# Strided casts shared with GpSimd, the state copy in eight pieces, and four kinds of preparation moved or cut smaller in a decode step

## The chip, the cores and the metric

The kernel runs on one core of a Trainium2 chip. The metric is the device time of one execution in microseconds (us). TensorE does the matrix products, VectorE, ScalarE and GpSimd the elementwise work, and SyncE's queue issues nearly all data transfers (DMAs), in order.

## What is computed

One layer of a decoder in one inference step: a prompt of 1024 tokens (8 tiles of 128) and 32 sample tokens (8 sequences of 4 tokens, each with 1024 cached positions). Two groups of attention heads stand in parallel, and their outputs are gated, projected and added to the input.

```python
u = h @ w_in            # all projections of the normalized input
# NSA: 8 query heads in 2 groups, three branches over shared keys/values
cmp_kv = compress_blocks(kv_c, cmp_pos, w_cmp1, w_cmp2)      # 32-row blocks, stride 16
logit_c = einsum(q, cmp_k) * scale + bias_c                   # compressed branch
logit_s = einsum(q, k_sel) * scale + bias_s                   # selected branch
logit_w = einsum(q, win_k) * scale + bias_w                   # window of 512
o_nsa = g0 * softmax(logit_c) @ v_c + g1 * softmax(logit_s) @ v_s + g2 * softmax(logit_w) @ v_w
# FoX: 8 heads, softmax with a forget term
logit = einsum(q, k) * scale + (cq - ck);  o_fox = softmax(logit) @ v
o = concat(o_nsa * silu(z_nsa), o_fox * silu(z_fox)) @ w_out
x = x + rms_norm(o, g_post);  x = x + (p @ w_pproj) * sigmoid(x @ w_pgate)
```

The outputs are the new `x` and the caches. One of these, the window state of the sample sequences, is mostly a copy: 508 of 512 rows of each sequence (4 MB in all) go from an input to an output unchanged.

## The kernel before

TensorE takes float32 operands in a rounded form, so an operand is split: `h` is the rounded value and `l` what is left of it, and products use both. `split` (L80) makes the pair: ScalarE casts `h` (L82), VectorE or GpSimd subtracts (L83).

The program has four stages. Up to 250 us it normalizes and transposes the input, makes the first projections and compresses the sequences' cached pages and then the prompt: `cmp_chunk` (L435 to L500) fills the tiles `X` for its products by `split`, from transposed pages (`ps_sc`, `ps_pt`), or for the prompt from `cT`, eight pieces of 64x512 with a step of 64 bytes between elements (L459, L461). From 250 to 615 us come the four FoX head pairs (`fox`, L745 to L800). Each makes its projections with `proj` (L225): four loads of 128 KB into `wr`, issued by SyncE, their split on ScalarE (L82) and GpSimd (L83), and 72 matmuls of 128x352 (L242), whose results ScalarE and VectorE evacuate (`os`, L509 and L510, for the gates; `os`, L521, for the NSA queries). Then eight query tiles follow, each with scores (`qk`, L632 and L633), a running minimum on VectorE and an exponential on ScalarE (`soft`, L638 and L640), transposes (L658) and products with the values (L684), and `mix_out`, which writes `d_mix` to memory (L725). At the end of the stage stand the projections for the selected and window branches, and the state copy (L917), one DMA behind the last FoX `d_mix`.

From 615 to 1005 us run the four NSA head pairs, `nsa(j)` (L966 to L1020), eight tiles each. `nsa_loads(j)` (L942) loads the queries `qr` (L946) and two bias tables `bias` (L950) of 520 KB each, finishes each table on GpSimd (L951 to L953), and splits selected keys, window keys and queries (`dup`, L614; L961 and L962) in whole rows of 1024 or 1088 columns. In a tile, the sums of the exponentials become factors `rs` on VectorE (L1009 to L1011), GpSimd scales five pieces of the scores with them (`norm`, L643) and VectorE one (`normv`, L646). Between tiles, steps of the sample tokens' attention are put in by `advance`: `sam_nsa`, whose scores are `s_s`, and twice `sam_fox` (L1181), which loads a small table `n4`, adds a mask (L1192), and makes `nbf` from it (`new_bias`, L1071) for its last scores. The sample queries are packed by 16 VectorE copies (L1054, L1055) when the last projection is done. From 1005 us on come the output projections; the change leaves them alone.

On every engine instructions run in the order that a scheduler chose from a timeline of its own; `tc.issue_after(ins)` adds the condition that an instruction stands behind `ins`.

## Time and profile before

| | us |
|---|---|
| median of 3 runs | 1276.54 (1274.31 to 1276.91) |
| profiled execution: its time | 1273.53 |
| profiled execution: its span | 1271.8 |
| TensorE busy in the span | 1170.5 (92%) |
| VectorE, ScalarE, GpSimd busy | 667.4, 606.5, 314.8 |

The span runs from the first instruction to the last of the profiled execution; its time has the 1.7 us around it as well. An engine's busy time leaves out what it waits. In the trace's rows an engine is PE (TensorE), PEld (TensorE's weight loads), DVE (VectorE), ACT (ScalarE), POOL (GpSimd) or SPq (the instructions with which SyncE issues DMAs); `out<-in` are the program's tile names, and the bracket at a row's end has the idle time of the engine before it and what ended that.

### The profile page before, as it was taken

The numbers are of one execution on the slowest core, as the hardware profiler recorded it, in microseconds if no ns is written. First come the engines' busy times: TensorE is split into PE (matmuls) and PEld (weight loads), VectorE is DVE, ScalarE is ACT, GpSimd is POOL, SyncE is SP. The second block draws the span as 40 slices with busy tenths as digits, with TensorE's granted clock in tenths as the row PEclk, the third lists the DMA queues.
The fourth block names the chain that finished last, engine by engine and source line by source line (L and its number), as shares of the span: only waits on it lengthen the run. The fifth ranks groups of instructions, "written<-read, shape, count | busy, mean of one in ns | idle before, by whom it ended". The sixth has DMA issues, their size and how long they took to land.

```text
span 1271.8 us, 23735 instructions
## 1 busy us (share of the span) xinstructions
PE 1170.5 (92%) x8106; PEld 979.6 (77%) x8106; DVE 667.4 (52%) x2062; ACT 606.5 (48%) x1415; POOL 314.8 (25%) x433
## 2 busy tenths in 40 slices
PE   3899989999999999999978799899989797999998
PEld 3798879998899898988856567674764576877776
DVE  4614455325646566463467577775655745442222
ACT  7724453244544545453356577775675742231121
POOL 2511100222322222221132323322222514131112
PEclk8999989999999999999989999899999898999999
DMA  7535311328222313223551535545645475432221
GB/s 244 134 94 142 87 49 50 92 71 243 81 68 57 97 48 100 58 73 122 178 157 34 178 90 188 175 151 202 218 148 187 142 249 156 166 141 83 72 76 38
DMA packets 142731, 157.04 MB, mean 123 GB/s; under 512 B 16586, under 2 KB 109546, under 8 KB 142418
## 3 DMA queue, kind: packets, MB, share of 16 engines
q1 hardware_dynamic: 141378, 151.06, 38.7%
q10 hardware_dynamic: 1152, 4.19, 0.9%
q8 instruction: 64, 1.05, 0.3%
q14 instruction: 57, 0.47, 0.1%
q0 software_dynamic: 80, 0.26, 0.1%
HBM read 128.30 MB, written 36.38 MB: 129 GB/s over the span
## 4 chain that ended last, share of the span: by engine, by line
PE 64%; issue 9%; DMA 8%; DVE 6%; ACT 6%; POOL 3%; SPq 3%; POOLq 0%; ACTq 0%; DVEq 0%
PE ps_fl L242 20%; PE ps_sc L1313 9%; PE ps_pt L658 5%; DMA wr<-in_w_in_dram 3%; PE ps_pv L706 3%; PE ps_pv L684 3%; PE ps_sc L632 3%; PE ps_fl L1313 3%; PE ps_sc L633 2%; DVE s L638 2%; ACT s L640 2%; PE ps_sv L1250 2%; PE ps_pt L1313 2%; PE ps_pt L1215 1%; PE ps_sv L468 1%
## 5 line engine op out<-in xcount | busy, mean ns | idle before, releaser
L242 PE MATMUL ps_fl<-ht,wh 128*128 128x352 f32 x1440 | 369.2, 329 | 4.6 <-DVE os L510 2.9
L242 PEld LDWEIGHTS ps_fl<-ht,wh 128*128 128x128 f32 x1440 | 256.2, 190 | 9.9 <-DVE os L510 3.2
L242 PE MATMUL ps_fl<-ht,wl 128*128 128x352 f32 x720 | 236.5, 328 | 0.0
L640 ACT ACTIVATE s<-s,m 128x640 f32<-128x640 f32 (+8 forms) x256 | 164.6, 644 | 53.6 <-DVE m L638 50.7
L83 POOL TENSOR_TENSOR wl<-wr,wh 128x256 fp32r<-128x256 f32 x120 | 89.4, 751 | 263.1 <-ACT wh L82 261.6
L643 POOL TENSOR_SCALAR s<-s,rs 128x64 f32<-128x64 f32 (+8 forms) x160 | 93.4, 604 | 216.8 <-DVE rs L1011 132.7
L242 PEld LDWEIGHTS ps_fl<-ht,wl 128*128 128x128 f32 x720 | 137.0, 190 | 1.1 <-issue 0.3
L658 PE MATMUL ps_pt<-cst,s 128*128 128x128 f32 x816 | 126.9, 284 | 4.3 <-DVE s L94 1.9
L632 PE MATMUL ps_sc<-kh,q 128*128 128x320 f32 (+12 forms) x304 | 116.1, 386 | 13.8 <-DVE m L638 8.6
L638 DVE CUSTOM_DVE_ANT_0 s<-ps_sc,bias 128x128 f32<-128x128 f32 (+10 forms) x224 | 79.9, 388 | 77.9 <-PE ps_pv L712 22.5
L658 PEld LDWEIGHTS ps_pt<-cst,s 128*128 128x128 f32 x816 | 98.5, 145 | 19.9 <-issue 6.1
L93 ACT ACTIVATE s<-ps_pt 128x512 f32<-128x512 f32 (+2 forms) x165 | 87.1, 542 | 51.5 <-PE ps_pt L658 39.1
L633 PE MATMUL ps_sc<-kl,q 128*128 128x320 f32 (+12 forms) x304 | 101.2, 336 | 1.5 <-DVE kl L621 1.5
L638 DVE CUSTOM_DVE_ANT_0 s<-ps_sc,bias,m 128x320 f32<-128x320 f32 (+10 forms) x168 | 87.1, 524 | 7.3 <-PE ps_sc L633 2.9
L632 PEld LDWEIGHTS ps_sc<-kh,q 128*128 128x128 f32 x304 | 58.5, 192 | 41.5 <-DVE m L638 16.1
L82 ACT CAST wh<-wr 128x256 fp32r<-128x256 f32 x120 | 47.6, 404 | 70.0 <-PE ps_fl L242 42.6
L778 POOL TENSOR_TENSOR mc<-bias,cst 128x128 f32<-128x128 f32 x64 | 30.2, 477 | 147.7 <-DVE m L638 133.7
L94 DVE COPY s<-ps_pt 128x512 f32<-128x512 f32 (+2 forms) x83 | 48.7, 587 | 33.4 <-PE ps_pt L658 29.3
L633 PEld LDWEIGHTS ps_sc<-kl,q 128*128 128x128 f32 x304 | 59.1, 194 | 3.0 <-DVE kl L621 1.7
L646 DVE TENSOR_SCALAR s<-s,rs 128x128 f32<-128x128 f32 (+7 forms) x96 | 56.1, 612 | 1.8
L1313 PE MATMUL ps_sc<-fwh,xh 128*128 128x512 f32 x128 | 50.8, 397 | 2.1 <-ACT xh L82 2.1
L1313 PE MATMUL ps_sc<-fwl,xh 128*128 128x512 f32 x128 | 50.1, 391 | 0.0
(444 smaller groups left out, 2164.6 us busy)
## 6 DMA issues: line engine op xcount, KB each, us to landing
kp<-in_cache_fox_kv_dram SPq DMA_DIRECT2D x64, 256.0 KB
vp<-in_cache_fox_kv_dram SPq DMA_DIRECT2D x64, 256.0 KB
wr<-in_w_in_dram SPq DMA_DIRECT2D x120, 128.0 KB
pg<-in_cache_cmp_kv_dram SPq DMA_DIRECT2D x64, 128.0 KB
pg<-in_cache_slc_kv_dram SPq DMA_DIRECT2D x64, 128.0 KB
d_g<-d_r SPq DMA_DIRECT2D x1, 4800.0 KB
...
```

The source lines that it names most:

```text
L83: (l_eng or nc.vector).tensor_tensor(l, src, h.bitcast(F32), op=OP.subtract)
L93: return nc.scalar.activation(out, in_, AF.Copy, scale=1.0 if scale is None else scale)
L94: return nc.vector.tensor_copy(out, in_)
L242: nc.tensor.matmul(ps[:, :CH], lhsT=w[k // 2][:, k % 2], rhs=HT[k][:, hl, s], start=n == 0, stop=n == 3 * KD - 1)
L632: nc.tensor.matmul(out, lhsT=qi, rhs=ks[0][:, k0:k0 + n], start=True, stop=False)
L633: nc.tensor.matmul(out, lhsT=qi, rhs=ks[1][:, k0:k0 + n], start=False, stop=True)
L638: nc.vector.tensor_tensor_reduce(o, p, bi, scale=-1.0, scalar=BIG if x == 0 else m, op0=OP.add, op1=OP.min, accum_out=m)
L640: nc.scalar.activation(s_ap, s_ap, AF.Exp, scale=-1.0, bias=m, accum_out=ssum)
L643: nc.gpsimd.tensor_scalar(s_ap, s_ap, r, 0.0, op0=OP.mult, op1=OP.add)
L646: nc.vector.tensor_scalar(s_ap, s_ap, r, None, op0=OP.mult)
L658: nc.tensor.transpose(ps[:, (2 * x + a) * 128:(2 * x + a + 1) * 128], S[:, a, (b0 + x) * 128:(b0 + x + 1) * 128], ident)
L1313: nc.tensor.matmul(o, lhsT=a[al][:, k], rhs=w[k][wl][:, c * 512:(c + 1) * 512], start=k == 0 and x == 0, stop=k == nk - 1 and x == 2)
```

## The change

Six parts. (1) Half of the prompt's strided casts, those with r = 1, go from ScalarE to GpSimd. (2) The state copy becomes eight DMAs of 520 KB, one sequence each, issued behind the `d_mix` of tiles 2 and 5 of each FoX head pair. (3) The sample queries take 12 VectorE copies instead of 16, and are to stand behind norms of NSA tiles 2, 3 and 5 of the first head pair. (4) The GpSimd operations on the bias tables of head pair j are issued behind the last norm of tile 6 of head pair j - 1. (5) The small table's add and `new_bias` stand behind the minimum of the third chunk (c == 2). (6) The query tiles are allocated ahead of the keys', and keys and queries are split in four pieces of 256 (or 272) columns, one after another.

```diff
@@ -77,9 +77,12 @@
     zero1 = cpool.tile([128, 1], F32, name="zero1")
     nc.vector.memset(zero1, 0.0)
 
-    def split(h, l, src, scale=None, l_eng=None):
+    def split(h, l, src, scale=None, l_eng=None, h_eng=None):
         if scale is None:
-            nc.scalar.copy(h, src)
+            if h_eng is None:
+                nc.scalar.copy(h, src)
+            else:
+                h_eng.tensor_copy(h, src)
             (l_eng or nc.vector).tensor_tensor(l, src, h.bitcast(F32), op=OP.subtract)
         else:
             nc.scalar.activation(h, src, AF.Copy if isinstance(scale, float) else AF.Identity, scale=scale)
@@ -458,7 +461,7 @@
                         else:
                             sv = cTs[e][g * 64:(g + 1) * 64, :T].rearrange("p (s j r) -> p r j s", r=2, j=8)[:, r]
                         dv = [X[hl][r * 64:(r + 1) * 64, :, s:s + 64] for hl in range(2)]
-                        split(dv[0], dv[1], sv)
+                        split(dv[0], dv[1], sv, h_eng=nc.gpsimd if b == NB and r else None)
             ps = mm_tile(("pv", "sv")[e])
             n = 0
             for k in range(16):
@@ -611,14 +614,14 @@
         proj(c0, ev)
         return qs
 
-    def dup(src, a, n):
+    def dup(src, a, n, hl=None, x0=0):
         pr, op = slice(64 * a, 64 * a + 64), slice(64 - 64 * a, 128 - 64 * a)
-        h = st.tile([128, 1088], F32R, name="kh", tag="st")
-        l = st.tile([128, 1088], F32R, name="kl", tag="st")
-        nc.scalar.copy(h[pr, :n], src[pr, :n])
-        nc.scalar.copy(h[op, :n], src[pr, :n])
-        nc.vector.tensor_tensor(l[pr, :n], src[pr, :n], h[pr, :n].bitcast(F32), op=OP.subtract)
-        nc.vector.tensor_tensor(l[op, :n], src[pr, :n], h[pr, :n].bitcast(F32), op=OP.subtract)
+        h, l = hl or [st.tile([128, 1088], F32R, name=f"k{x}", tag="st") for x in "hl"]
+        c = slice(x0, x0 + n)
+        nc.scalar.copy(h[pr, c], src[pr, c])
+        nc.scalar.copy(h[op, c], src[pr, c])
+        nc.vector.tensor_tensor(l[pr, c], src[pr, c], h[pr, c].bitcast(F32), op=OP.subtract)
+        nc.vector.tensor_tensor(l[op, c], src[pr, c], h[pr, c].bitcast(F32), op=OP.subtract)
         return h, l
 
     def cuts(n):
@@ -639,8 +642,10 @@
                                            accum_out=m)
         nc.scalar.activation(s_ap, s_ap, AF.Exp, scale=-1.0, bias=m, accum_out=ssum)
 
+    later, normed = {}, {}
+
     def norm(s_ap, r):
-        nc.gpsimd.tensor_scalar(s_ap, s_ap, r, 0.0, op0=OP.mult, op1=OP.add)
+        return nc.gpsimd.tensor_scalar(s_ap, s_ap, r, 0.0, op0=OP.mult, op1=OP.add)
 
     def normv(s_ap, r):
         nc.vector.tensor_scalar(s_ap, s_ap, r, None, op0=OP.mult)
@@ -796,6 +801,10 @@
             mix = ap_.tile([128, 128], F32, name="mix", bufs=2)
             pv_pairs(mm_tile("pv"), S, V, i + 1, mix)
             mix_out(mix, 4 + j, i)
+            if i in (2, 5):
+                b = 2 * j + i // 5
+                with tc.issue_after(last_mix[0].ins):
+                    nc.sync.dma_start(wso[b, 0:508], wst[b, 4:512])
 
     for j in range(4):
         if j == 1:
@@ -913,8 +922,6 @@
                 live.remove(x)
 
 
-    with tc.issue_after(last_mix[0].ins):
-        nc.sync.dma_start(wso[:, 0:508], wst[:, 4:512])
     ksT = kvp.tile([128, 64 + TA], F32, name="ksT", tag="kv")
     kwT = kvp.tile([128, 64 + TA], F32, name="kwT", tag="kv")
     VS = ap_.tile([128, NT, 128], F32, name="VS", tag="V", bufs=2)
@@ -948,18 +955,35 @@
         for a in range(2):
             t = ap_.tile([128, 1288], F32, name="bias", bufs=BB)
             nc.sync.dma_start(t[:, :1040], raw(d_g, (2 * j + a) * RW + 131, [[8 * RW - 1, 128], [1, 1040]]))
-            nc.gpsimd.tensor_tensor(t[:, 1040:1168], t[:, 384:512], cst[:, CO["WM"]], op=OP.add)
-            nc.gpsimd.tensor_copy(t[:, 1168:1232], t[:, 31:1040:16])
-            nc.gpsimd.memset(t[:, 1232:1288], NEG)
             G.append(t)
+
+        def rest():
+            for t in G:
+                nc.gpsimd.tensor_tensor(t[:, 1040:1168], t[:, 384:512], cst[:, CO["WM"]], op=OP.add)
+                nc.gpsimd.tensor_copy(t[:, 1168:1232], t[:, 31:1040:16])
+                nc.gpsimd.memset(t[:, 1232:1288], NEG)
+        if j:
+            with tc.issue_after(normed[j - 1, NT - 2].ins):
+                rest()
+        else:
+            rest()
+        q = [st.tile([128, 1088], F32R, name=f"q{a}", tag="st") for a in range(2)]
         if j % 2 == 0:
-            grp["s"] = dup(ksT, g, 1088)
-            grp["w"] = dup(kwT, g, T)
-        q = [st.tile([128, 1088], F32R, name=f"q{a}", tag="st") for a in range(2)]
-        for a in range(2):
-            pr, op = slice(64 * a, 64 * a + 64), slice(64 - 64 * a, 128 - 64 * a)
-            nc.scalar.copy(q[a][pr, :T], qr[pr])
-            nc.vector.tensor_tensor(q[a][op, :T], qr[pr], q[a][pr, :T].bitcast(F32), op=OP.subtract)
+            grp["s"] = [st.tile([128, 1088], F32R, name=f"ks{a}", tag="st") for a in range(2)]
+            grp["w"] = [st.tile([128, 1088], F32R, name=f"kw{a}", tag="st") for a in range(2)]
+
+        def parts():
+
+            for x in range(4):
+                if j % 2 == 0:
+                    dup(ksT, g, 272, grp["s"], x * 272)
+                    dup(kwT, g, 256, grp["w"], x * 256)
+                c = slice(x * 256, x * 256 + 256)
+                for a in range(2):
+                    pr, op = slice(64 * a, 64 * a + 64), slice(64 - 64 * a, 128 - 64 * a)
+                    nc.scalar.copy(q[a][pr, c], qr[pr, c])
+                    nc.vector.tensor_tensor(q[a][op, c], qr[pr, c], q[a][pr, c].bitcast(F32), op=OP.subtract)
+        parts()
         return q, grp["s"], grp["w"], G
 
     def nsa(j, loads, tiles=range(NT)):
@@ -1012,7 +1036,11 @@
             for a in range(2):
                 norm(s3[:, 64 * a:64 * a + 64], rs[:, 3 * a:3 * a + 1])
                 (normv, norm)[a](S[:, a, :n], rs[:, 3 * a + 1:3 * a + 2])
-                norm(S[:, a, n:n + nw], rs[:, 3 * a + 2:3 * a + 3])
+                x = norm(S[:, a, n:n + nw], rs[:, 3 * a + 2:3 * a + 3])
+            normed[j, i] = x
+            with tc.issue_after(x.ins):
+                for f in later.pop((j, i), ()):
+                    f()
             mix = ap_.tile([128, 128], F32, name="mix", bufs=2)
             V = [VS[:, b, gs] for b in range(i + 1)] + [VW[:, i + 1 - w + b, gs] for b in range(w)]
             pv_shared(mm_tile("pv"), S, s3, V, i + 1 + w, g, mix)
@@ -1049,10 +1077,20 @@
     qs_n = sp.tile([128, NB, 32], F32, name="qs_n")
     nc.gpsimd.memset(qs_f, 0.0)
     nc.gpsimd.memset(qs_n, 0.0)
-    for h in range(8):
+
+    def sample_q_n():
+        for y in range(2):
+            for a in range(2):
+                dst = qs_n[64 * y:64 * y + 64].rearrange("p b (h t) -> p h b t", t=4)[:, 4 * y + a:4 * y + 4:2]
+                src = qsam[64 * a:64 * a + 64, 2 * y:2 * y + 2].rearrange("p h (b t) -> p h b t", t=4)
+                nc.vector.tensor_copy(dst, src)
+
+    def sample_q_f(h):
         pr, hs = slice(64 * (h % 2), 64 * (h % 2) + 64), slice(h * 4, h * 4 + 4)
         nc.vector.tensor_copy(qs_f[pr, h // 2, :, hs], qsam[pr, 4 + h // 2].rearrange("p (b t) -> p b t", t=4))
-        nc.vector.tensor_copy(qs_n[64 * (h // 4):64 * (h // 4) + 64, :, hs], qsam[pr, h // 2].rearrange("p (b t) -> p b t", t=4))
+    later[0, 2] = [sample_q_n]
+    later[0, 3] = [lambda: [sample_q_f(h) for h in range(4)]]
+    later[0, 5] = [lambda: [sample_q_f(h) for h in range(4, 8)]]
     sb = sp.tile([128, 1028], F32, name="sb")
     for b in range(4):
         nc.sync.dma_start(sb[32 * b:32 * b + 32], d_sb)
@@ -1189,8 +1227,6 @@
             nc.sync.dma_start(nk[32 * bl:32 * bl + 32], raw(d_cs, bs[bl] * 1024, [[8192, 8], [0, 4], [1, 1024]]))
         n4 = sp.tile([128, 4], F32, name="n4", bufs=2)
         nc.sync.dma_start(n4, raw(d_cn, gq * 128, [[4, 32], [0, 4], [1, 4]]))
-        nc.vector.tensor_tensor(n4, n4, cst[:, CO["CM4"]], op=OP.add)
-        nb_ = new_bias("nbf", n4, gq)
         kf = I["cache_fox_kv"]
         q = [[qs_f[:, j, b] for j in range(4)] for b in bs]
         s = sp.tile([128, 1056], F32, name="s_s", tag="s_s", bufs=2)
@@ -1221,8 +1257,12 @@
                                          start=j == 0, stop=j == 3) for j in range(4) for bl in range(4)], ev)
             yield 2
             ps = sc
-            nc.vector.tensor_tensor_reduce(s[:, c * 256:(c + 1) * 256], ps[:, :256], nk[:, c * 256:(c + 1) * 256],
-                                           scale=-1.0, scalar=BIG if c == 0 else m, op0=OP.add, op1=OP.min, accum_out=m)
+            x = nc.vector.tensor_tensor_reduce(s[:, c * 256:(c + 1) * 256], ps[:, :256], nk[:, c * 256:(c + 1) * 256],
+                                               scale=-1.0, scalar=BIG if c == 0 else m, op0=OP.add, op1=OP.min, accum_out=m)
+            if c == 2:
+                with tc.issue_after(x.ins):
+                    nc.vector.tensor_tensor(n4, n4, cst[:, CO["CM4"]], op=OP.add)
+                    nb_ = new_bias("nbf", n4, gq)
         ps = mm_tile("pt")
         score4(ps[:, :32], q, [[kt_f[:, j] for j in range(4)]] * 4)
         nc.vector.tensor_tensor_reduce(s[:, 1024:1056], ps[:, :32], nb_, scale=-1.0, scalar=m, op0=OP.add, op1=OP.min,
```

Three places in the orders follow, before and after.

On ScalarE, around the prompt's casts, before (`cT` is the prompt's transposed input, `ps_pt` a transposed page):

```order
L82 CAST X<-posT 128x8x2
L82 CAST X<-cT 64x8x64 x4
L82 CAST X<-posT 128x8x2
L82 CAST X<-cT 64x8x64 x4
L82 CAST X<-ps_pt 64x8x64
L485 ACT_TABLE_LOAD
L485 ACTIVATE th<-ps_pv,bt 128x256
L521 ACTIVATE os<-ps_fl 128x352
```

and now:

```order
L83 CAST X<-posT 128x8x2
L83 CAST X<-cT 64x8x64 x2
L83 CAST X<-posT 128x8x2
L83 CAST X<-cT 64x8x64 x2
L83 CAST X<-ps_pt 64x8x64
L488 ACT_TABLE_LOAD
L488 ACTIVATE th<-ps_pv,bt 128x256
L524 ACTIVATE os<-ps_fl 128x352
```

Each run of four casts from `cT` is a run of two; the four others stand on GpSimd in one block, between two runs of weight subtracts.

On VectorE, behind the evacuation `os` of the last gate projection, up to the scaling that uses `rs`; before:

```order
L719 SCALAR_TENSOR_TENSOR mix<-ps_pv,mix 64x128
L1055 COPY qs_n<-qsam 64x8x4
L1010 RECIPROCAL rs_7770<-rs_7770 128x6
L1055 COPY qs_n<-qsam 64x8x4
L1054 COPY qs_f<-qsam 64x8x4
L1055 COPY qs_n<-qsam 64x8x4
L1054 COPY qs_f<-qsam 64x8x4
L1055 COPY qs_n<-qsam 64x8x4
L1054 COPY qs_f<-qsam 64x8x4
L1055 COPY qs_n<-qsam 64x8x4
L1054 COPY qs_f<-qsam 64x8x4
L1011 TENSOR_TENSOR rs_7770<-rs_7770,gates 128x6
```

and now:

```order
L1090 COPY qs_f<-qsam 64x8x4 x4
L1086 COPY qs_n<-qsam 64x2x8x4 x3
L516 TENSOR_SCALAR zsam<-os 128x32
L1086 COPY qs_n<-qsam 64x2x8x4
L1090 COPY qs_f<-qsam 64x8x4 x2
L1033 TENSOR_SCALAR rs_7813<-sums_7786 128x6
L1090 COPY qs_f<-qsam 64x8x4 x2
L724 SCALAR_TENSOR_TENSOR mix<-ps_pv,mix 64x128
L1034 RECIPROCAL rs_7813<-rs_7813 128x6
L1035 TENSOR_TENSOR rs_7813<-rs_7813,gates 128x6
L724 SCALAR_TENSOR_TENSOR mix<-ps_pv,mix 64x128
L651 TENSOR_SCALAR s<-s,rs_7813 128x256
```

The sixteen copies were strewn among the steps to `rs`. The twelve stand at the same place, all ahead of the second step to `rs`.

On GpSimd, at the end of the first head pair, from behind tile 6's scalings to those of tile 7 and of the sample scores `s_s`; before:

```order
L953 MEMSET bias 128x56 x2
L951 TENSOR_TENSOR bias<-bias,cst 128x128
L952 COPY bias<-bias 128x64
L643 TENSOR_SCALAR s_9004<-s_9004,rs_9068 128x64
L643 TENSOR_SCALAR s<-s,rs_9068 128x640
L643 TENSOR_SCALAR s_9004<-s_9004,rs_9068 128x64
L643 TENSOR_SCALAR s<-s,rs_9068 128x1024
L643 TENSOR_SCALAR s<-s,rs_9068 128x640
L643 TENSOR_SCALAR s_s<-s_s,ssr 128x544
L951 TENSOR_TENSOR bias<-bias,cst 128x128
L952 COPY bias<-bias 128x64
```

and now:

```order
L962 TENSOR_TENSOR bias<-bias,cst 128x128
L963 COPY bias<-bias 128x64
L964 MEMSET bias 128x56
L962 TENSOR_TENSOR bias<-bias,cst 128x128
L963 COPY bias<-bias 128x64
L964 MEMSET bias 128x56
L648 TENSOR_SCALAR s_9043<-s_9043,rs_9107 128x64
L648 TENSOR_SCALAR s<-s,rs_9107 128x640
L648 TENSOR_SCALAR s_9043<-s_9043,rs_9107 128x64
L648 TENSOR_SCALAR s<-s,rs_9107 128x1024
L648 TENSOR_SCALAR s<-s,rs_9107 128x640
L648 TENSOR_SCALAR s_s<-s_s,ssr 128x544
```

Before, the operations on the third pair's two tables stood ahead of tile 7's scalings and behind `s_s`. Now the block here is that of the second pair's tables; the third pair's block stands behind tile 6 of the second pair.

## Rows read from the trace of the kernel before

**Rows 1.** The page: busy time, share of the span and instructions of each engine.

```profile
PE 1170.5 (92%) x8106; PEld 979.6 (77%) x8106; DVE 667.4 (52%) x2062; ACT 606.5 (48%) x1415; POOL 314.8 (25%) x433
```

**Rows 2.** Busy us (and count) per engine by stretch; clock, DMA share, GB/s.

```profile
250.00:615.00 365.00, 356.86 (x2620) 329.63 (x2619) 190.68 (x583) 170.79 (x388) 89.24 (x150) 1.00 0.34 97
...
615.00:1005.00 390.00, 348.36 (x2832) 248.68 (x2831) 256.99 (x1002) 248.34 (x646) 109.72 (x182) 0.96 0.49 156
```

**Rows 3.** TensorE's waits: total us, times, the longest.

```profile
PE ps_sc L632 <- DVE m L638: 8.6, 18, 1.2
```

**Rows 4.** Two stretches at half the granted clock; columns as in rows 2.

```profile
172.06:182.29 10.23, 7.71 (x33) 6.76 (x34) 6.23 (x17) 4.38 (x10) 2.83 (x4) 0.50 0.34 95
...
622.62:626.02 3.40, 3.40 (x14) 3.40 (x13) 2.46 (x3) 3.07 (x5) 0.49 (x1) 0.50 0.18 62
```

**Rows 5.** Timeline, the prompt's casts (start us, us, engine, line, operation).

```profile
167.18 4.29 ACT L82 CAST X<-cT 64x512 fp32r<-64x512 f32 x4
...
167.58 0.60 PE L453 MATMUL ps_pt<-cst,pg 128*128 128x128 f32 x4
...
169.44 3.16 DVE L83 TENSOR_TENSOR X<-cT,X 64x512 fp32r<-64x512 f32 x3
...
174.26 0.69 PE L326 MATMUL ps_fl<-lf,cst 128*128 128x64 f32 x2 [5.65 <-ACT os L521]
```

**Rows 6.** Timeline around the state copy.

```profile
596.12 0.77 SPq L917 DMA_DIRECT2D out_win_kv_sample_dram<-in_state_win_kv_dram  x1
...
604.57 3.39 SPq L230 DMA_DIRECT2D wr<-in_w_in_dram  x3
...
620.37 0.41 ACT L82 CAST wh<-wr 128x256 fp32r<-128x256 f32 x1 [10.41 <-DMA wr<-in_w_in_dram]
...
621.75 0.43 PE L242 MATMUL ps_fl<-ht,wh 128*128 128x352 f32 x1 [2.93 <-DVE os L510]
```

**Rows 7.** Timeline, sample queries and the scalings behind them.

```profile
642.51 0.36 DVE L1054 COPY qs_f<-qsam 64x32 f32<-64x32 f32 x2
...
645.57 2.02 POOL L643 TENSOR_SCALAR s<-s,rs 128x64 f32<-128x64 f32 x5 [3.81 <-DVE rs L1011]
...
646.71 0.48 PE L694 MATMUL ps_pt<-cst,s 128*128 128x128 f32 x1 [4.42 <-POOL s L643]
```

**Rows 8.** Timeline around the small table's add.

```profile
678.60 0.16 DVE L1192 TENSOR_TENSOR n<-n,cst 128x4 f32<-128x4 f32 x1 [2.02 <-DMA n<-d_cn]
...
679.42 1.09 PE L1112 MATMUL ps_pt<-cst,pg 128*128 128x128 f32 x8 [2.38 <-DVE kt L94]
```

**Rows 9.** Timeline, third head pair's bias table and tile 7's scalings.

```profile
718.13 0.17 DVE L1011 TENSOR_TENSOR rs<-rs,gates 128x6 f32<-128x6 f32 x1
...
722.10 0.46 POOL L951 TENSOR_TENSOR bias<-bias,cst 128x128 f32<-128x128 f32 x1 [5.54 <-DMA bias<-d_g]
...
722.76 3.25 POOL L643 TENSOR_SCALAR s<-s,rs 128x64 f32<-128x64 f32 x5
...
725.98 0.72 POOL L643 TENSOR_SCALAR s_s<-s_s,ssr 128x544 f32<-128x544 f32 x1
...
726.75 0.66 PE L1080 MATMUL ps_pt<-cst,s_s 128*128 128x128 f32 x4 [3.75 <-POOL s_s L643]
```

**Rows 10.** Groups by line and shape: casts and subtracts of whole and cut rows.

```profile
L961 ACT CAST q<-qr x8: 1038/1044/1051, 622.4 to 807.9; 64x1024 fp32r<-64x1024 f32 x8
...
L82 ACT CAST wh<-wr 128x256 fp32r<-128x256 f32 x120 | 47.6, 404 | 70.0 <-PE ps_fl L242 42.6
...
L962 DVE TENSOR_TENSOR q<-qr,q 64x1024 fp32r<-64x1024 f32 x8 | 9.9, 1238 | 3.4 <-ACT q L961 3.2
```

**Rows 11.** GpSimd's strided copy of the bias table, and its slowest case.

```profile
L952 POOL COPY bias<-bias x8: 278/286/1279, 511.0 to 813.5; 128x64 f32<-128x64 f32 x8
...
809.17 3.87 DVE L962 TENSOR_TENSOR q<-qr,q 64x1024 fp32r<-64x1024 f32 x3
...
811.91 1.28 POOL L952 COPY bias<-bias 128x64 f32<-128x64 f32 x1
```

## The prediction

> **What bounds the kernel now.** I read the page first. TensorE works 1170.5 of 1271.8 us [rows 1], so most of what can be had is what stands between its instructions. By stage, the FoX heads leave it idle 8 of 365 us, the NSA heads 42 of 390, and the NSA stage is also where VectorE and ScalarE are each busy some 250 us [rows 2]. So I listed TensorE's waits, and its single idle stretches over 0.8 us. Part of the NSA stage's idle time is 18 waits of about half a microsecond for VectorE's row minimum, 8.6 us in all [rows 3]; the change doesn't aim at them. But five long single stalls stand in places that the diff touches: 5.65 us at 168.6 [rows 5], 2.93 at 618.8 [rows 6], 4.42 at 642.3 [rows 7], 2.38 at 677.0 [rows 8] and 3.75 at 723.0 [rows 9].
>
> Each stall costs a second time. A table by stretches of the granted clock shows 0.50, the 1.2 GHz level, just behind four of them: 10.23 us long near 172, and 3.40 us near 622.6 [rows 4], with two more of 3.4 us and as much work near 680.6 and 728.4. Matmul work done there would have taken half as long at 2.4 GHz, so such a stretch costs about half its TensorE busy time: 3.9, 1.7, 1.7 and 1.7 us. I count this where a stall goes entirely.
>
> **Casts.** ScalarE casts eight strided 64x512 pieces, the last four in 4.29 us [rows 5]. Behind them, in its order, stand the cast of a transposed cache page, a table load, and the projection's evacuation `os`, for which TensorE waits until 174.26. The change gives four of the eight to GpSimd, which has nothing else to do there. Four casts at 1.07 us are 4.3 us off ScalarE, but that page's four transposes end only at about 168.2. So its cast can start at 168.3 instead of 171.5, and `os` ends 3.2 us earlier: the stall shrinks from 5.65 to about 2.45. Of the slow stretch's 3.9 us I take half, 2.0, since a stall remains. Sum: -5.2.
>
> What a GpSimd cast of 64x512 costs, no row shows. From below, GpSimd's 128x544 scaling takes 0.72 us [rows 9]; from above, its strided 64-column copy takes 0.286 [rows 11], and eight times that is 2.3. Four of them take 2.9 to 9.2 us. Started at 162.6, they are done by 165.5 to 171.8, and VectorE began the last of its subtracts on them at 171.5. I take 1.2 us each, nearer the scaling's row, since both go over some 500 columns; at 2.3 each, TensorE's next stream would wait and 1 to 2 us of the gain would be gone.
>
> Against this part speaks what one row shows. GpSimd's copy took 0.28 us seven times and 1.28 us once: at 811.91, while VectorE ran three subtracts with both inputs in SBUF until 813.04; the copy ended at 813.19 [rows 11]. The casts now stand beside eight such subtracts of 1.0 to 1.1 us each [rows 5]. The Trainium skill says the same as a rule ("SBUF — State Buffer", section "Who interferes with whom"): a VectorE instruction with two SBUF inputs and a GpSimd instruction that reads SBUF exclude each other, for the whole instruction. By that rule the term is the second rival's -1.2, and not -5.2. I stay with -5.2: with four casts less on ScalarE the subtracts can start earlier, which pays for part of a lock, and only one of eight copies showed one.
>
> **State copy.** One 4 MB DMA is issued at 596.12 [rows 6]. Weight loads issued from 604.57 on are cast only at 620.37, after a wait of 10.41 us on ScalarE; `os` and its VectorE half stand in order behind that, and TensorE gets its buffer at 621.75, after 2.93 us. Removed: -2.9, and -1.7 of slow clock. SP issues the eight new pieces in the FoX heads, behind the mix of tiles 2 and 5; three of them stand between the third and the fourth weight load of a projection. The whole stood in the way for at most 24 us (596.12 to 620.37), so a piece of 520 KB does for at most 3. TensorE is busy 98% there [rows 2], so weights arrive well before they are used. Bounds: 0 (all hidden) and 3.0 each, 24 us. I take +1.0, near the lower, since the FoX stage uses a third of the DMA engines. If that cover goes, the third rival follows.
>
> **Sample queries.** Sixteen VectorE copies (of which [rows 7] show the first two) stand among the steps to `rs`, which five GpSimd scalings, and then TensorE, wait for. The change packs them into twelve and hangs them behind norms of later tiles. But those norms run on GpSimd and the copies on VectorE, and the new order shows the copies still behind the same `os`, now ahead of `rs` in one block. Counted in that order at 0.18 to 0.2 us each, `rs` is ready at 645.5 to 645.8; before, the scalings started at 645.57. So this part doesn't do what it says: 0, with bounds of -2 and +1.
>
> **Small table.** The add on `n` waited 2.02 us for its load on VectorE, with a copy `kt` behind it for which TensorE waited [rows 8]. The add now stands behind the third chunk's minimum, long after the load. TensorE gets the 2.4 us, and 1.7 of clock: -4.1. The table's reader is the last chunk; nothing is queued behind it there.
>
> **Bias table.** GpSimd waited 5.54 us for a bias load at 722.10, and tile 7's five scalings and `s_s` stood behind it; TensorE waited 3.75 us for `s_s` [rows 9]. In the new order the third pair's tables are finished behind tile 6 of the second pair, most of a head pair after that load; in the old place stand the second pair's tables, loaded long before. Then the scalings start when `rs` is there, at 718.3, and `s_s` ends by 718.3 + 3.25 + 0.72 = 722.3, before TensorE asks at 723.0. -3.7 and -1.7: -5.4. The fourth pair's tables, near 812 us, cost nothing before, since the scalings there waited for `rs` anyway: 0.
>
> **Splits.** Sixteen ScalarE casts and sixteen subtracts become 64 and 64. A 64x1024 cast takes 1.04 us, a 128x256 one 0.40; a 64x1024 subtract 1.24 [rows 10]; a 256-column one I estimate at 0.42: the cast's ratio of 0.39 would give 0.48, and without a fixed part it would be 0.31. Work: ScalarE 64 x 0.404 - 16 x 1.044 = +9 us, VectorE 64 x 0.42 - 16 x 1.238 = +7. In return the first pieces can be used earlier and nothing waits behind 1.2 us. But the order keeps them together: up to eleven subtracts for a query in a row, where there were three. Bounds: -3 (the waits of 1.69 and 0.92 us near 805 to 808 vanish with their slow clock) and +9 (all of ScalarE's work on the path). I take +3, a third of the upper, since the row minimum's waits end last in this stage [rows 3] and pieces on VectorE delay them.
>
> **Sum.** -5.2 - 4.6 + 1.0 + 0 - 4.1 - 5.4 + 3.0 = -15.3 against the profiled execution's 1273.53, which is its span of 1271.8 and 1.7 around it: 1258.2. That execution is 3.0 under the median of the runs, 1276.54, and I set the forecast beside the median: **1261.2 us**. About 0.2% (2.5 us) can be told from no change.
>
> **Rivals.** First, *given back in the NSA stage*. With the stalls gone, ScalarE and VectorE, whose busy time there rises by 9 and 7 us, set the pace; the table's and the bias's 9.5 us are lost again in half-microsecond waits. For it: the 8.6 us of row-minimum waits [rows 3]. Against it: TensorE is still busier than either by over 80 us [rows 2]. Casts and copy remain, less 3 for the splits: 1276.5 - 5.2 - 3.6 + 3.0 = 1270.7; with half given back, 1266.
>
> Second, *exclusion of casts and subtracts*. If each GpSimd cast holds VectorE off for its 1.2 us, the last subtract, which ended at 172.60, ends some 3 to 4 us later than I count, and the stream that needs it takes over the stall: the term falls to -1.2, and the time is 1265.2.
>
> Third, on the other side, *the pieces hurt the weight loads*. The 4 MB copy cost TensorE 2.9 + 1.7 us when it met one projection's loads [rows 6]. If each of the eight pieces does what the whole did, that is 37 us in place of 1.0: 1261.2 + 36 = 1297. Without the pieces the change stands at -16.3, so it decides from 2.0 us per piece on. Against it: a piece is an eighth of the copy, and the FoX loads have slack.
>
> **How the numbers follow.** The forecast has 0.60 (1254 to 1268), the first rival 0.22, the second 0.10, the third 0.08. The range 1250 to 1272 takes in the forecast and its unknown terms, the second rival and most of the first; the third and the tails, under 0.2, lie outside. Slower by over 0.2% is the third: 0.07. Within 0.2% fall 0.06, from the first and third rivals. Faster: 0.87.
>
> **What would show it.** Right: TensorE's stall near 168 is under 3 us; none of a microsecond or more before the `n` add's `kt` or before `s_s`; VectorE's `os` near 620 without a wait for weights; the stall behind the query copies is still about 4 us. TensorE's idle time in the FoX stage grows by under 2 us. Wrong: FoX waits of TensorE for weights after each piece; GpSimd casts or subtracts beside them at twice 1.0 us; new waits for `q`, `kh` or the minimum between 615 and 1005 that sum to over 6 us.

## The result and the profile after

The changed kernel takes 1267.97 us, the median of 5 runs (1262.52 to 1269.66), beside 1276.54 of the kernel before (1274.31 to 1279.28). The ratio is 0.9916 with a 95% interval of 0.9894 to 0.9938: 0.8% faster. Forecast were 1261.2 us, with 1250 to 1272 as the range. So the sign and the range held, and of the 15.3 us of the sum 8.6 arrived. Run again later the kernel gave a ratio of 0.9919 (0.9891 to 0.9946). The profiled execution took 1269.66 us, the most of the five, while that of before took less than all five beside it.

The page's busy times, in the order of [rows 1]:

```profile
PE 1169.2 (92%) x8106; PEld 980.6 (77%) x8106; DVE 677.4 (53%) x2106; ACT 610.0 (48%) x1459; POOL 320.2 (25%) x437
```

TensorE has the same work as before. VectorE has 10 us more and ScalarE 3.5. The stages, as in [rows 2]:

```profile
250.00:615.00 365.00, 356.11 (x2596) 331.63 (x2597) 190.81 (x582) 173.11 (x402) 89.31 (x147) 0.99 0.35 100
...
615.00:1005.00 390.00, 352.31 (x2874) 252.51 (x2875) 268.50 (x1057) 258.56 (x688) 110.88 (x186) 0.96 0.49 155
```

The NSA stage has only 3.9 us less idle time of TensorE, 37.7 us instead of 41.6, although the three stalls taken out of it were 9 us (2.93, 2.38 and 3.75). ScalarE and VectorE are 10 and 11.5 us busier there. The list of TensorE's waits over the whole span (total, times, longest) shows what stands there now. Of its last four rows, L329 (L326 before) had 5.6 us, and the other three are new; three of the four belong to the casts near 170 us:

```profile
PE ps_pt L699 <- POOL s L648: 13.8, 8, 4.8
...
PE ps_sc L635 <- DVE m L641: 6.2, 16, 1.0
...
PE ps_pt L840 <- ACT ktw L96: 2.3, 1, 2.3
...
PE ps_sv L471 <- ACT X L83: 1.9, 1, 1.9
...
PE ps_fl L329 <- ACT os L524: 1.5, 1, 1.5
...
PE ps_pv L494 <- DVE qsam L527: 1.2, 1, 1.2
```

Around the casts, the answer to [rows 5]. The timeline's columns are start, duration, engine, line, operation, and idle time before:

```profile
162.50 5.75 POOL L85 CAST X<-cT 64x512 fp32r<-64x512 f32 x4 [13.00 <-PE ps_pv L471]
...
162.57 2.26 ACT L83 CAST X<-cT 64x512 fp32r<-64x512 f32 x2
...
163.70 3.64 DVE L86 TENSOR_TENSOR X<-cT,X 64x512 fp32r<-64x512 f32 x2
...
169.45 0.46 ACT L524 ACTIVATE os<-ps_fl 128x352 f32<-128x352 f32 x1
...
169.96 0.43 PE L329 MATMUL ps_fl<-lf,cst 128*128 128x64 f32 x2 [1.49 <-ACT os L524]
...
172.68 0.58 PE L471 MATMUL ps_sv<-X,w1h 128*128 128x258 f32 x1 [1.95 <-ACT X L83]
...
174.73 0.69 PE L494 MATMUL ps_pv<-th,w 128*64 128x128 f32 x4 [1.25 <-DVE qsam L527]
```

The evacuation on ScalarE is 4.3 us earlier, and TensorE's wait for it is 1.49 us instead of 5.65. But GpSimd's four casts took 5.75 us, 1.44 each. The shortest, median and longest of the eight subtracts, in ns, were 999, 1022 and 1053 before, and now

```profile
L86 DVE TENSOR_TENSOR X<-cT,X x8: 994/1037/1924, 163.7 to 177.1; 64x512 fp32r<-64x512 f32 x8
```

The two that ran beside the casts took 3.64 us in all. Two new stalls of 1.95 and 1.25 us follow: the first for a cast on ScalarE that itself waited for VectorE's `X`, the second for VectorE's `qsam`. The three together are 4.7 us.

The copy pieces (first row: shortest, median and longest issue in ns, and the first and last start in us), and the gate evacuation that answers to [rows 6]:

```profile
L807 SPq DMA_DIRECT2D out_win_kv_sample_dram<-in_state_win_kv_dram x8: 521/529/589, 316.3 to 581.2; - x8
...
612.36 0.46 ACT L512 ACTIVATE os<-ps_fl 128x352 f32<-128x352 f32 x1 [3.55 <-PE ps_fl L245]
...
612.85 0.52 DVE L513 SCALAR_TENSOR_TENSOR os<-os,ps_fl 128x352 f32<-128x352 f32 x1 [2.88 <-ACT os L512]
```

No weights are waited for there any more. The three places that answer to [rows 7], [rows 8] and [rows 9]:

```profile
642.00 2.08 POOL L648 TENSOR_SCALAR s<-s,rs 128x64 f32<-128x64 f32 x5 [4.69 <-ACT mix L723]
...
643.24 0.47 PE L699 MATMUL ps_pt<-cst,s 128*128 128x128 f32 x1 [4.77 <-POOL s L648]
...
673.72 1.09 PE L1150 MATMUL ps_pt<-cst,pg 128*128 128x128 f32 x8 [0.19 <-DVE kt L97]
...
718.38 0.71 POOL L648 TENSOR_SCALAR s_s<-s_s,ssr 128x544 f32<-128x544 f32 x1
...
721.08 0.60 PE L1118 MATMUL ps_pt<-cst,s_s 128*128 128x128 f32 x4
```

Behind the query copies the stall is 4.77 us, where it was 4.42. Behind the small table it is 0.19. The last two rows show the sample scores scaled at 718.38 and their transposes at 721.08 without a wait; the scalings ahead of them no longer stood behind a bias load.

And a new stall of 2.30 us. This is ScalarE's order ahead of it, with two pieces of key casts between two evacuations:

```profile
705.68 0.58 ACT L96 ACTIVATE s<-ps_pt 128x512 f32<-128x512 f32 x1
...
706.29 0.42 ACT L621 CAST ks<-ksT 64x272 fp32r<-64x272 f32 x1
...
706.73 0.42 ACT L622 CAST ks<-ksT 64x272 fp32r<-64x272 f32 x1
...
707.05 0.59 ACT L96 ACTIVATE ktw<-ps_pt 128x512 f32<-128x512 f32 x1
...
708.82 0.57 ACT L96 ACTIVATE ktw<-ps_pt 128x512 f32<-128x512 f32 x1
...
709.44 1.96 PE L840 MATMUL ps_pt<-ktw,qs_n 128*32 128x512 f32 x8 [2.30 <-ACT ktw L96]
```

Behind it stands a slow stretch (columns as in [rows 2]) that costs half of its 8.66 us of TensorE work:

```profile
708.55:718.79 10.24, 8.66 (x46) 5.10 (x48) 5.23 (x18) 4.59 (x11) 4.08 (x6) 0.50 0.45 158
```

### The profile page after: what moved, and what is told of

Its sections match the earlier page's. It is cut to its first block, busy times and chain, and to the rows that moved or that the text cites. A ratio compares the mean times of both kernels' runs of the same rounds, so it can differ in the third digit from the quotient of the medians.

```text
span 1267.9 us, 23844 instructions
## 1 busy us (share of the span) xinstructions
PE 1169.2 (92%) x8106; PEld 980.6 (77%) x8106; DVE 677.4 (53%) x2106; ACT 610.0 (48%) x1459; POOL 320.2 (25%) x437
## 3 DMA queue, kind: packets, MB, share of 16 engines
q8 instruction: 64, 1.05, 0.3%
## 4 chain that ended last, share of the span: by engine, by line
PE 67%; DMA 8%; ACT 8%; issue 7%; DVE 6%; POOL 3%; SPq 1%; POOLq 0%; DVEq 0%; ACTq 0%
PE ps_fl L245 21%; PE ps_sc L1353 9%; PE ps_pt L663 5%; PE ps_pv L711 4%; PE ps_sc L635 3%; PE ps_pv L689 3%; PE ps_fl L1353 3%; ACT s L643 2%; PE ps_sc L636 2%; PE ps_pt L1353 2%; PE ps_sv L1290 2%; DVE s L641 2%; PE ps_sv L471 2%; DMA wr<-in_w_in_dram 1%; DMA d_mix<-mix 1%
## 5 line engine op out<-in xcount | busy, mean ns | idle before, releaser
L723 ACT ACTIVATE mix<-ps_pv 64x128 f32<-64x128 f32 x64 | 17.3, 270 | 67.8 <-PE ps_pv L717 50.2
L1353 PE MATMUL ps_sc<-fwh,xl 128*128 128x512 f32 x128 | 49.7, 396 | 0.0
L643 ACT ACTIVATION_READ_ACCUMULATOR s<-s,m 128x1 f32 x256 | 48.1, 188 | 0.0
L635 PE MATMUL ps_sc<-ks,q 128*128 128x288 f32 (+8 forms) x112 | 44.6, 399 | 2.7 <-DVE m L641 1.6
```

Of the source, the lines that this page charges most:

```text
L635: nc.tensor.matmul(out, lhsT=qi, rhs=ks[0][:, k0:k0 + n], start=True, stop=False)
L643: nc.scalar.activation(s_ap, s_ap, AF.Exp, scale=-1.0, bias=m, accum_out=ssum)
L1353: nc.tensor.matmul(o, lhsT=a[al][:, k], rhs=w[k][wl][:, c * 512:(c + 1) * 512], start=k == 0 and x == 0, stop=k == nk - 1 and x == 2)
```

## The experiments

Twelve kernels ran: eight of them undo or redo one or two parts of the change, two put parts on the kernel before, one repeats the changed kernel, one measures a price. A ratio is to the kernel before on the same chip.

Since executions of one kernel differ by 7 us and more, a part of 1 to 5 us is better read from the traces by stages. For every matmul of TensorE, the start in a run's trace minus the start of the same matmul in the trace of before was taken. The table gives the median over the matmuls that start, in the trace of before, in 262 to 270 us, 440 to 480, 745 to 765, 920 to 945 and 1220 to 1260, each minus the median over 110 to 150 us, ahead of all changes (by there the profiles stand 1.0 us earlier to 2.9 later than that of before; up to 1.0 us of it is there at the first matmuls). Negative is earlier. The last column tells in which order the scheduler put the output projections behind 1005 us, which no edit touches: whether the sample rows' product comes near 1050 us, as before, or near 1110 (other). In d1 and f1 it stands as before, with the order behind 1125 us a little different.

| run | 262 | 440 | 745 | 920 | 1220 | ratio, 95% interval | order |
|---|---|---|---|---|---|---|---|
| changed kernel | -0.2 | 3.6 | -7.2 | -5.2 | -3.9 | 0.9916, 0.9894 to 0.9938 | as before |
| c1_same | -0.2 | 1.6 | -9.3 | -8.5 | -6.5 | 0.9919, 0.9891 to 0.9946 | as before |
| c2_queries | -0.7 | 1.6 | -8.8 | -7.7 | -11.1 | 0.9870, 0.9840 to 0.9901 | other |
| c3_nocasts | -0.1 | 2.5 | -11.0 | -9.7 | -12.5 | 0.9872, 0.9842 to 0.9902 | other |
| c4_nosplits | -1.2 | 2.7 | -13.0 | -12.9 | -12.4 | 0.9864, 0.9834 to 0.9894 | as before |
| d1_pieces | 0.1 | 2.6 | 0.2 | 0.5 | 1.4 | 0.9960, 0.9939 to 0.9980 | nearly as before |
| d2_onecopy | -1.4 | 0.4 | -6.4 | -5.5 | -8.9 | 0.9895, 0.9873 to 0.9918 | other |
| d3_nolate | -1.8 | -0.5 | -7.6 | -7.0 | -6.8 | 0.9949, 0.9930 to 0.9967 | as before |
| d4_two_undone | -0.5 | 1.7 | -14.9 | -14.5 | -17.9 | 0.9836, 0.9814 to 0.9859 | other |
| f1_three_parts | -0.3 | 2.3 | -12.3 | -11.3 | -9.9 | 0.9885, 0.9864 to 0.9907 | nearly as before |
| f2_keyswhole | -1.5 | 0.2 | -13.6 | -13.5 | -16.1 | 0.9853, 0.9829 to 0.9877 | other |
| f3_querieswhole | -0.7 | 1.6 | -9.2 | -7.5 | -7.0 | 0.9913, 0.9892 to 0.9934 | other |
| f4_nosub | -3.5 | 0.2 | -10.2 | -9.5 | -9.5 | one run | as before |

All entries are against the one profiled execution of before (1273.53 us, where the medians beside the runs are 1276.5 to 1279.3), so they show 3 to 6 us less gain than the ratios. Compare rows with rows. The changed kernel, c1_same and f4_nosub have the same order on every engine from 440 to 920 us and gain 8.7, 10.1 and 9.7 us there, so one reading is good to about 1 us. In the other runs the scheduler also moved instructions in that stage, which adds to a difference what no edit asked for.

**The changed kernel again.** No edit.

> The changed kernel again, unchanged, as a measure for the three others and for how far two profiles of one program differ. Theory (what separates executions of one program is the granted clock): its time lies between 1262 and 1270, and a profile that is some us shorter than the first one's 1269.66 shows that much less time at 0.50 of the clock, half of it in us. Rival (waits differ from run to run): the time at 0.50 is the same within 3.4 us and the idle time of TensorE differs.

1268.67 us median; the profile has 1269.75, against 1269.66, with a granted clock of 0.975 against 0.972 over the span. The same stalls stand at the same places within 0.3 us (1.48, 1.94 and 1.53 near 171; 4.77 near 639; 2.30 near 708). What differs is the clock behind them: 6.8 us at half instead of 10.2 behind the 4.77 stall, and none at 289 and 350, where the first had 3.4 each. In all the time at half the clock is 66.2 us against 73.2. But this profile had lost 2.6 us on the first one by 50 us: 0.6 before its first matmul (17.05 against 16.41), and 1.3 over a slow stretch from 39.9 to 46.7 that the first doesn't have. So slow stretches and the start change between executions. Five of the six times lie between 1262 and 1270, as the theory had it (the sixth is 1270.85), but the profile with less time at half the clock wasn't shorter, so its second half missed. The rival, the same time at half the clock within 3.4 us, missed too.

**The query copies really moved.** The hook was the last scaling, on GpSimd; here it is VectorE's:

```diff
-                (normv, norm)[a](S[:, a, :n], ...)
+                y = (normv, norm)[a](S[:, a, :n], ...)
+                v = v if a else y
-            with tc.issue_after(x.ins):
+            with tc.issue_after(v.ins):
```

> The changed kernel with the sample query copies hung behind VectorE's scaling of tiles 2, 3 and 5 instead of GpSimd's, so that they do move. Theory (the copies set when the factors are ready): the stall of 4.77 us near 638 falls to under 2.5, the slow stretch of 10.24 us behind it shrinks, and the time falls by 4 to 8 us against the changed kernel. Rival (the stall is of its making in any case, since the factors wait for the last evacuation): the stall stays above 4 us and the time within 2 us.

The copies now stand behind the scalings. The wait for the scalings is 2.87 us and not 4.77, but a second one has come up right behind it:

```profile
643.59 0.33 PE L699 MATMUL ps_pt<-cst,s 128*128 128x128 f32 x1 [2.87 <-POOL s L648]
...
646.18 0.16 DVE L1099 TENSOR_TENSOR sbw<-sb,cst 128x4 f32<-128x4 f32 x1 [3.25 <-DMA sb<-d_sb]
...
647.54 1.12 PE L711 MATMUL ps_pv<-s,VW 128*64 128x256 f32 x4 [2.50 <-DVE s L97]
```

VectorE is held by the add on `sb`, whose load hadn't landed: 3.25 us, most of which the copies used to cover. 2.87 + 2.50 is 5.4 us; in the changed kernel it is 4.77 + 0.94. By the table the run stands at -7.7 behind the NSA stage, between the two profiles of the changed kernel (-5.2 and -8.5). So the copies' move is worth nothing, and most of the 6 us of its median come behind 1005 us, from the other order of the output projections. The size fit the theory, the place does not (the stall is above its 2.5), and the rival is right about the mechanism's worth though not about the stall.

**All casts on ScalarE.**

```diff
-                        split(dv[0], dv[1], sv, h_eng=nc.gpsimd if b == NB and r else None)
+                        split(dv[0], dv[1], sv)
```

> The changed kernel with all eight strided casts on ScalarE again. My sum's theory (the part is worth 5.2 us): the time rises by 4 to 6 us. Rival (GpSimd's casts and VectorE's subtracts exclude each other, so the part gives most of it back): VectorE's eight subtracts go back from 1.0 to 1.8 us each to 1.0 to 1.1, and the time rises by 0 to 2 us.

VectorE's first four subtracts take 4.39 us again, one every 1.10:

```profile
164.40 4.39 DVE L86 TENSOR_TENSOR X<-cT,X 64x512 fp32r<-64x512 f32 x4 [0.70 <-ACT X L83]
```

The stall of 5.63 us is back, in place of 1.48 + 1.94 + 1.53. At 262 us this kernel stands at -0.1, and the eight profiles with the casts on GpSimd and the subtracts in place at -0.2 to -1.8, mean -0.9; the five without the part (before among them) at +0.1 to -0.5, mean -0.2. So the part is worth 0.8 us, where my sum had 5.2 and the rival up to 2. The whole got faster by 7 us against the changed kernel, which neither expected. The output projections stand in the other order, and in the NSA stage TensorE's order differs too: behind the same key casts the stall near 707 us is 0.74 us instead of 2.30, and the slow stretch is 6.8 us long instead of 10.2.

```profile
707.06 1.09 PE L840 MATMUL ps_pt<-ktw,qs_n 128*32 128x512 f32 x8 [0.74 <-ACT ktw L96]
```

**Whole rows again.**

```diff
-            for x in range(4):
+            for x in range(1):
                 if j % 2 == 0:
-                    dup(ksT, g, 272, grp["s"], x * 272)
-                    dup(kwT, g, 256, grp["w"], x * 256)
-                c = slice(x * 256, x * 256 + 256)
+                    dup(ksT, g, 1088, grp["s"], 0)
+                    dup(kwT, g, T, grp["w"], 0)
+                c = slice(0, T)
```

> The changed kernel with keys and queries split in whole rows again (16 casts and 16 subtracts instead of 64 and 64). My sum's theory (the pieces cost 3 us): the time falls by 1 to 5 us, and the stalls of 2.30 us near 707 and 1.3 us near 798 and 801 go or shrink. First rival (the whole shortfall of some 7 us against my sum is given back by the pieces): it falls by 6 us or more. Second rival (the pieces pay): it rises by 1 to 4 us.

1262.04 us. From 440 to 920 us it gains 15.5 us on before, the changed kernel 8.7 and 10.1: the splits cost 6.1 us there, in the order of the output projections that the changed kernel has too. The stall near 707 is gone. That is twice my term, and at the edge of the first rival's 6. A second pair gives less: from c3_nocasts (12.2) to d4_two_undone (16.2), both with all casts on ScalarE, it is 4.0. So the splits cost 4 to 6 us.

**The copy in pieces alone, and the copy in one piece.** The first adds this part to the kernel before, as shown; the second takes it out of the changed one, the reverse:

```diff
+            if i in (2, 5):
+                b = 2 * j + i // 5
+                with tc.issue_after(last_mix[0].ins):
+                    nc.sync.dma_start(wso[b, 0:508], wst[b, 4:512])
-    with tc.issue_after(last_mix[0].ins):
-        nc.sync.dma_start(wso[:, 0:508], wst[:, 4:512])
```

> The kernel before with the state copy in eight pieces and nothing else. My sum's theory: -2.9 us of stall and -1.7 of slow clock near 620, +1.0 for the pieces in the FoX heads: the time falls by 2 to 5 us against the kernel before; the same matmuls at the end of the FoX heads (near 480) start 0 to 1.5 us later than before. Rival (the third one of the prediction, small): the pieces make the FoX heads 2 to 4 us longer, as they were in all five traces with pieces so far, and the part is worth 0 to 2 us. The output projections keep the order of before here, so nothing comes from there.

> The changed kernel with the one 4 MB copy in its old place. If the pieces lengthen the FoX heads, the same matmul near 480 starts 1.5 to 3.5 us earlier than in the changed kernel, counted from the first projections; if not, within 1 us. The wait for weights near 610 to 620 comes back: +4 to +7 us there. The output projections stand in the other order here (that of the run without GpSimd casts), which should give back 4 to 6 us behind 1005; by stages up to 920 us it is 1 to 6 us slower than the changed kernel.

Alone it gives 0.9960 (0.9939 to 0.9980), some 5 us, and 2.1 by stages (440 to 920). With one copy, the wait behind the copy's landing is back, 4.77 us, not for weights as expected but for a query split whose `qr` was queued behind it:

```profile
627.70 0.53 PE L635 MATMUL ps_sc<-ks,q 128*128 128x192 f32 x1 [4.77 <-DVE q L983]
```

From 440 to 920 us that kernel gains 5.9 us and not 9.4 (the changed kernel's mean): the part is worth 3.5, as summed (-4.6 + 1.0). At 440 us the kernel with the pieces alone is 2.6 us late, more than the 1.5 that I had allowed and in the rival's range. But the FoX heads (262 to 440) are 1.8 us longer than in the trace of before even with one copy, and 1.2 to 3.9, 2.5 in the mean, in the twelve with pieces. So most of this isn't the pieces. A slow stretch near 346 to 350 is in eleven of the thirteen profiles, the one with one copy among them, and not in that of before; what sets it off isn't shown. Some 0.7 us are left for the pieces, if anything; my +1.0 stands, and its bound of 24 us was far too wide.

**The two delays undone.** The `n` add and the tables' GpSimd operations in their old places (the lines of the change, reversed).

> The changed kernel with the small table's add and the bias tables' finishing in their old places. My sum's theory: 9.5 us in all, so the time rises by 7 to 11 us, and stalls of about 2.4 us (for kt behind the add) and 3.7 us (for s_s behind the tables) are back. Rival (given back in the NSA stage by other waits): it rises by 1 to 5 us. The output projections keep the order of the changed kernel.

1271.81 us, 4 us (0.32%) more than the changed kernel. The add's wait is back, longer than before, and TensorE's with it:

```profile
669.96 0.36 DVE L1226 TENSOR_TENSOR n<-n,cst 128x4 f32<-128x4 f32 x1 [2.44 <-DMA n<-d_cn]
...
670.95 0.72 PE L635 MATMUL ps_sc<-ks,q 128*128 128x416 f32 x1 [3.06 <-DVE m L641]
```

But the wait for `s_s` is only 1.22 us. The third pair's bias loads are issued 2.4 us ahead of the last step to `rs` here; in d1_pieces, without the other parts of the change, 0.1 us behind it, and the wait for `s_s` is 4.42 us. First d3_nolate, then d1_pieces:

```profile
710.74 0.81 SPq L957 DMA_DIRECT2D bias<-d_g  x2
...
720.44 0.66 PE L1114 MATMUL ps_pt<-cst,s_s 128*128 128x128 f32 x4 [1.22 <-POOL s_s L648]
...
717.12 0.34 SPq L952 DMA_DIRECT2D bias<-d_g  x1
...
725.85 1.12 PE L1082 MATMUL ps_pt<-cst,s_s 128*128 128x128 f32 x4 [4.42 <-POOL s_s L643]
```

So other parts of the change (which of them isn't separated) had already taken most of this wait away. By stages the two delays are worth 2.9 us here (6.5 from 440 to 920 against 9.4), so the rival's size holds inside the changed kernel.

**Casts and splits undone together.** Both edits of above.

> The changed kernel with all strided casts on ScalarE and keys and queries split in whole rows: only the eight copy pieces, the small table, the bias tables, the twelve query copies and the allocation order are left of the change. Theory: the splits cost some 6 us in the NSA stage, the casts nothing, and the output projections stand in the other order, worth 4 to 6: 1254 to 1260 us, 1 to 2% under the kernel before. Rival (the two single undoings gained what they did by the order of the output projections alone): 1261 to 1264, as each of them.

1257.56 us, ratio 0.9836: as the theory had it, and with f2_keyswhole the fastest of all kernels here.

**Three parts alone on the kernel before**: copy pieces, small table, bias tables.

> The kernel before with three parts alone: the copy in eight pieces, the small table's add and the bias tables' finishing later. The output projections keep the order of before. My sum's theory: -4.6 + 1.0 - 4.1 - 5.4 = -13.1 us, so about 1266 where the kernel before has 1279: ratio 0.987 to 0.992. Rival (other waits take their place whatever the splits do, as 4 us for the two delays in the changed kernel suggest): -5 to -9 us, ratio 0.993 to 0.996. If the first holds, the splits are what takes the gain back in the changed kernel.

0.9885 (0.9864 to 0.9907), that is 14.7 us, with the sample rows' product placed as before. The sum's 13.1 holds. By stages, from 440 to 920 it gains 13.6, the copy alone 2.1: the two delays are worth 11.5 us in a kernel without the other parts, where the sum had 9.5 (the ratios, 0.9885 against 0.9960, say 9.6). With them they are worth 2.9. What takes most of the gain back stands in the next runs.

**Keys whole, queries in pieces; and the reverse.**

```diff
-            for x in range(4):
-                if j % 2 == 0:
-                    dup(ksT, g, 272, grp["s"], x * 272)
-                    dup(kwT, g, 256, grp["w"], x * 256)
+            if j % 2 == 0:
+                dup(ksT, g, 1088, grp["s"], 0)
+                dup(kwT, g, T, grp["w"], 0)
+            for x in range(4):
```

> The changed kernel with keys split in whole rows and only queries in pieces. If the key pieces near 702 to 710 are what costs (six casts and eight subtracts ahead of ktw), the stall of 2.30 us near 707 and the slow stretch behind it are gone and the stretch from 665 to 745 is 4 to 6 us shorter than in the changed kernel. If the query pieces cost, it is within 1.5 us of the changed kernel there. The output projections stand in the faster order (4 us), so the whole is 1258 to 1261 us in the first case and 1263 to 1266 in the second.

> The changed kernel with queries split in whole rows and only keys in pieces; the counterpart of the run before. If the key pieces cost, the 2.30 us stall near 707 stays and the time is 1263 to 1266 us (the output projections stand in the faster order here too); if the query pieces cost, 1258 to 1261.

1257.68 us with whole keys and 1266.42 with whole queries, both in the other order: it is the key pieces that cost. ScalarE's order with whole keys, at the place shown above for the changed kernel:

```profile
702.22 0.57 ACT L96 ACTIVATE s<-ps_pt 128x512 f32<-128x512 f32 x1
...
702.69 0.59 ACT L96 ACTIVATE ktw<-ps_pt 128x512 f32<-128x512 f32 x1
...
704.31 0.59 ACT L96 ACTIVATE ktw<-ps_pt 128x512 f32<-128x512 f32 x1
...
704.95 1.96 PE L840 MATMUL ps_pt<-ktw,qs_n 128*32 128x512 f32 x8 [1.28 <-ACT ktw L96]
```

The evacuation of `ktw` follows that of `s` by 0.47 us instead of 1.37, since two key casts of 0.42 no longer stand between them, and the stall is 1.28 instead of 2.30. I had expected it to go; what is left stands behind two exponentials between the two `ktw` rows, which the changed kernel has there too. The slow stretch behind it is a third as long:

```profile
704.89:708.31 3.42, 3.36 (x22) 2.01 (x23) 1.83 (x7) 2.43 (x6) 0.00 (x0) 0.50 0.01 2
```

10.24 us with 8.66 of work against 3.42 with 3.36 is (8.66 - 3.36) / 2 = 2.7 us. With 1.0 of stall that is 3.7 of the 4.3 us by which the stretch from 440 to 920 is shorter (13.7 against 9.4). The 1.0 and the 2.7 belong to this order of TensorE: in c2_queries, c3_nocasts and d2_onecopy the same two casts stand ahead of `ktw`, and the stall is 0.73 to 0.74.

**What a GpSimd cast costs by itself.** The prompt's subtracts are left out (the low halves are zeros that VectorE writes without reading).

> The changed kernel with the eight subtracts of the prompt's chunk left out (VectorE fills the low halves with zeros instead, an instruction that reads nothing), so the products of that chunk use the high halves alone. If subtracts and GpSimd's casts exclude each other, the four casts fall from 1.10 to 1.69 us each (5.75 in all) to 1.0 to 1.2 each without spread; if a cast of this form simply takes 1.4 us on GpSimd, they stay at 1.3 to 1.5 each.

```profile
163.42 4.59 POOL L465 CAST X<-cT 64x512 fp32r<-64x512 f32 x4 [13.00 <-PE ps_pv L475]
...
L465 POOL CAST X<-cT x4: 1086/1103/1135, 163.4 to 166.9; 64x512 fp32r<-64x512 f32 x4
```

1.09 to 1.14 us each, against 1.10, 1.39 (median) and 1.69 with the subtracts. The same kernel stands at -3.5 us at 262, and with the subtracts at -0.2 to -1.8. So the casts' lengthening comes from the subtracts beside them. The 2.6 us between -3.5 and the mean of -0.9 are at most what this takes back: the eight subtracts' own time is gone here too, and ScalarE evacuates `os` ahead of the table load, so that TensorE has one stall of 3.03 us in place of the three. A run that separates these wasn't made.

## Why the prediction was right, and where it was wrong

The sign, the range and most mechanisms held; of the size a little over half came, and two terms, casts and splits, account for the rest.

- **What bounds it.** Long single stalls with a slow stretch behind them: right. Taking three of them out gave 14.7 us on the kernel before, where the sum had 13.1. The table of slow stretches had one more, 6.83 us behind the stall of the query copies, which the prediction leaves out; it put that part at 0, so nothing hung on it.
- **Casts, -5.2.** Wrong size: -0.8. The step that failed was "with four casts less on ScalarE the subtracts can start earlier, which pays for part of a lock": the first one started at the same time (163.70, before 163.73) and the last one ended at 178.1 instead of 172.6. The price of "1.2 us each" was right for a cast alone, 1.1 us. Beside the subtracts both are longer, the casts up to 1.69 and the subtracts up to 1.92 us, close to the twice 1.0 us that I had named as a sign of being wrong. The stall for `os` itself fell further than I had it, to 1.49 and not 2.45, since the cached page whose cast I let wait until 168.3 was cast at 167.18, so it had been transposed earlier than I read. The loss is in the two stalls that followed. The trace of before had the lengthening in one row (1.28 instead of 0.28 us [rows 11]), and the second rival's -1.2 is near what came. From the first subtract's start to the last cast's end the changed kernel took 4.6 us, for work that takes 5.4 us one after another and 3.3 us side by side (an estimate, from a cast of 1.1 and a subtract of 1.05). The rule of the Trainium skill ("SBUF — State Buffer", section "Who interferes with whom") that a VectorE instruction with two SBUF inputs and a GpSimd instruction that reads SBUF exclude each other agrees with these numbers for the most part. It should have carried the term.
- **State copy, -3.6.** Right: 3.5 by stages inside the changed kernel, 2.1 on the kernel before, and 0.9960 alone. The third rival (pieces that hurt the weight loads) did not come: TensorE's idle time in 250 to 615 us is 8.9 us, against 8.1, and one copy in place of eight pieces makes the FoX heads only 0.7 us shorter.
- **Sample queries, 0.** Right, the stall is 4.77 us. Nor are they worth anything once moved: the next wait, for `sb`, was hidden under them.
- **Small table and bias, -4.1 and -5.4.** Right as the cost of these waits (9.6 to 11.5 us between d1_pieces and f1_three_parts), wrong as a part of the sum: with the other parts in, undoing both costs 2.9 to 4 us, since the wait for `s_s` is then 1.22 us and not 3.75. The sum took the terms as independent.
- **Splits, +3.** The mis-sized term: 4.0 to 6.1 by stages, within my bounds. I had the work right (256-column casts and subtracts took 0.40 and 0.42 us, as I had them; 272-column ones 0.42 and 0.44), and put "a third of the upper" on the path by a share. What mattered most was a place: the pieces of keys for the third head pair, cast ahead of `ktw` at 706, in an order of TensorE that then waits for it. They explain 3.7 us; where the rest arises isn't shown. The query pieces, of which I wrote "up to eleven subtracts in a row", cost little: undoing them alone moved nothing (f3 from 440 to 920: -9.1).
- **First rival**, gains given back in the NSA stage: it came in part, ScalarE and VectorE being busier by more than its 9 and 7 us, but as one stall with a slow stretch of 10 us and not as half-microsecond waits; those for the row minimum even fell, from 8.6 to 6.2 us.
- **The sum with the two measured terms**: -15.3 + 4.4 (casts) + 1.0 to 3.1 (splits) = -9.9 to -7.8, so 1266.6 to 1268.7 us, where 1267.97 and 1268.67 were measured. That it fits so well is partly luck, with terms that are read to about 1 us each and that overlap.
- **Not in the prediction**: the scheduler may reorder a stage that no edit touches. From 920 to 1220 us the order of before ends 0.1 us earlier to 2.0 later than in its own trace, the other one 2.6 to 3.4 earlier in five of six runs (0.4 later in the sixth). In the order of before the sample rows' product waits for `as` of VectorE:

```profile
1050.86 0.79 PE L1362 MATMUL ps_pv<-fwh,as 128*128 128x512 f32 x1 [7.19 <-DVE as L86]
```

The other order has no wait over 2.8 us there. The changed kernel kept the slower one, with 7.3 us at this place (before 6.9). Whether that order could be set by hand wasn't tried.
